# Neighbourhood attention in blocks of 8 rows by 16 columns, keys in chunks of 4 rows, and one value product for both row halves

## The chip, the core and the metric

One Trainium2 chip, one of its cores. Five engines run side by side, each from its own queue in order: TensorE (PE, with its weight loads shown as PEld), VectorE (DVE), ScalarE (ACT), GpSimd (POOL) and SyncE (SP, which here only issues DMAs; ACT and POOL issue some too). The metric is the device time of one execution in microseconds (us), the median of three runs.

## The reference, cut to what matters

One encoder layer on 1024 tokens of 1024 channels: an input projection, three branches (a Fourier mix, neighbourhood attention, attention into 256 memory tokens), a gated merge, an output projection, a LayerNorm, and then a mixture of 64 experts. The change is inside neighbourhood attention. The tokens are a grid of 16 rows by 64 columns; each of 8 heads has 64 channels; a query attends to a window of 8 rows by 16 columns that is clipped at the grid's edges, with a learned bias for each offset:

```
col_start = np.clip(cols - NA_COL_WIN // 2, 0, GRID_W - NA_COL_WIN)
...
def one_row(r):
    rs = jnp.clip(r - kr // 2, 0, rows - kr)
    k_win = k_rows[:, :, :, col_idx]; v_win = v_rows[:, :, :, col_idx]
    sc = jnp.einsum('bhcd,bhrckd->bhcrk', q_r, k_win) * scale + bias
    p = softmax over the 8 x 16 keys
    return jnp.einsum('bhcrk,bhrckd->bhcd', p, v_win)
```

## The kernel before

Everything is float32. Projections run as three products of split operands (high and low parts, `xh`, `xl`, `wh`, `wl`): method `job` issues 48 matmuls of 512 columns for each 128 output channels (L195), in two halves of 512 tokens; a `sink` takes each half out of PSUM. The projections wait in one list (`js`); `adv(n)` issues the next n of their matmuls, `finish(name)` issues all up to the end of one job. So projection matmuls of later work (gates, memory queries) fill PE between the steps of attention.

Method `na` runs the neighbourhood attention. First the four V jobs, whose sink (`v_sink`, L489) copies V out of PSUM (`vt`), turns it by transposes on PE (L503) and lays it into `V`. Then, for each pair of heads `hp`, the Q and K jobs; `q_sink` (L518, L519) splits Q into a high part by ACT and a low part by DVE, `k_sink` does so for K and copies halves by DMA. Then units: a unit is one head `a` of the pair and one block of 128 queries. Before, a block is 4 rows by 32 columns, and its keys are 8 or 11 rows by 40 columns; there are 64 units. A unit has these steps:

- `scores`: two matmuls over all of the block's keys (high and low K, L562) of 320 or 440 columns into a bank `s`; DVE adds bias and mask and takes the minimum (L568), ACT takes the exponential (L570), DVE the reciprocal and the product (L571, L572), into `sc`;
- `turned`: transposes of `sc` on PE (L583), one for each chunk of keys (3 rows, 2 rows or 1 row of 40 columns, so 120, 80 or 40 keys; 3, 3, 4, 4, 5, 5, 3, 3 of them for the eight units of a half row), into a bank `t`, and copies into `pt`, one for each size of chunk, by ACT and DVE in turn (`evac`, L151, L153);
- `values`, once for two units (both heads): for each chunk and each head one product of 128 columns with V as the stationary operand (L598), into a bank `o`. The two heads stand in different halves of the array's columns (64 each). The program has 240 such products; the trace shows each as two instructions.

Between `scores` and `turned` and after `turned` stand `adv(3)` each. `na_bias` loads the bias by a DMA on ACT's queue and POOL subtracts it from the masks (L540, L541), a half row ahead. `tile` schedules the whole program beforehand with its own estimates, so that the order in which instructions stand on an engine is not the order of the code.

What follows attention: the memory attention with the rest of the projections as filler, `merge`, `out_proj` with routing, and the experts, whose weights (64 times three of 2 MB) come by DMA.

Of the kernel before, what the change touches and what calls it, by code (L numbers as in the profile page):

```python
# [5 lines left out]
F32 = mybir.dt.float32  # L6
# [5 lines left out]
OP = mybir.AluOpType  # L12
# [7 lines left out]
KF = 516  # L20

# [14 lines left out]
def constants():  # L36
# [27 lines left out]
    q, kc = np.arange(32), np.arange(40)  # L64
    m = np.arange(-4, 8)
    i = np.arange(4)
    cm = np.zeros((2, 4, 32, 40))
    for h in range(2):
        cs = np.clip(32 * h + q - 8, 0, 48)
        cm[h] = np.where((24 * h + kc >= cs[:, None]) & (24 * h + kc < cs[:, None] + 16), 0.0, 1e30)  # L70
    rm = np.where((m >= i[:, None] - 4) & (m < i[:, None] + 4), 0.0, 1e30)
    c["nmask"] = cm.reshape(2, 128, 1, 40).astype(np.float32)
    mid = np.maximum(cm[:, :, :, None, :], rm[None, :, None, :11, None])
    c["nmask_mid"] = mid.reshape(2, 128, 11, 40).astype(np.float32)
# [3 lines left out]
def layout(i):  # L78
# [17 lines left out]
    q, kc, hf = np.arange(32), np.arange(40), np.arange(2)  # L96
    dc = np.clip((24 * hf[:, None, None] + kc) - (32 * hf[:, None, None] + q[:, None]) + 15, 0, 30)
    dr = np.arange(-4, 8) - np.arange(4)[:, None] + 7
    g = rpb[:, dr[None, :, None, :, None], dc[:, None, :, None, :]]
    a["rpb"] = np.ascontiguousarray(g.reshape(8, 2, 128, 12, 40))  # L100
# [22 lines left out]
class Dense:  # L123
# [304 lines left out]
    def fourier_merge(s, pool):  # L428
# [24 lines left out]
        for d in range(8):  # L453
# [14 lines left out]
            for b in range(2):  # L468
# [13 lines left out]
    CHUNKS = ((0, 3), (3, 3), (8, 3), (11, 3), (4, 2), (6, 2), (14, 2))  # L482

    BLOCKS = ((0, 8, ((0, 3), (1, 3), (5, 2))),
# [3 lines left out]

    def v_sink(s, f):  # L489
        def sink(half, p):  # L490
            v = s.N1.tile([128, 2, 320], F32, name="vt", bufs=2)
            for hf in range(2):
                s.evac(v[:, hf].rearrange("p (r c) -> p r c", c=40), p.rearrange("p (r c) -> p r c", c=64)[:, :, 24 * hf:24 * hf + 40])

            def later():
                V = s.V.rearrange("p (h c) f -> p h c f", h=2)
                for cs, K in (((0, 1), 120), ((4, 5), 80)) if half == 0 else (((2, 3), 120), ((6,), 80)):
                    q = s.bank("t")
                    n = len(cs)
                    for hf in range(2):  # L500
                        for i, c in enumerate(cs):
                            r = s.CHUNKS[c][0] - 8 * half
                            s.nc.tensor.transpose(q[:K, (n * hf + i) * 128:(n * hf + i + 1) * 128], v[:, hf, 40 * r:40 * r + K], s.ident)  # L503
                    s.evac(V[:K, :, cs[0]:cs[0] + n, f * 128:(f + 1) * 128],
                           q[:K, :2 * n * 128].rearrange("p (h c f) -> p h c f", h=2, c=n))
            return later
        return sink

    def q_sink(s, hp):
        def sink(half, p):  # L510
            nc = s.nc
            if half == 0:
                s.QS = s.N1.tile([128, 2, 2, 16, 32], FR, name="QS")
            for a in range(2):
                for h in range(2):
                    src = p[64 * a:64 * a + 64].rearrange("p (r h c) -> p h r c", h=2, c=32)[:, h]
                    hi, lo = s.QS[0:64, a, h, 8 * half:8 * half + 8], s.QS[64:128, a, h, 8 * half:8 * half + 8]
                    nc.scalar.activation(hi, src, AF.Copy, scale=-0.125)  # L518
                    nc.vector.scalar_tensor_tensor(lo, src, -0.125, hi.bitcast(F32), op0=OP.mult, op1=OP.subtract)  # L519
        return sink  # L520
# [14 lines left out]
    def na_bias(s, h, hf):  # L535
        nc, A, pool = s.nc, s.A, s.N1
        bt = pool.tile([128, 12, 40], F32, name="bt", bufs=4)
        bm = pool.tile([128, 11, 40], F32, name="bm", bufs=4)
        nc.scalar.dma_start(bt, A["rpb"][h, hf])
        nc.gpsimd.tensor_tensor(out=bm, in0=s.nmm[:, hf], in1=bt[:, 0:11], op=OP.subtract)  # L540
        nc.gpsimd.tensor_tensor(out=bt, in0=s.nm[:, hf].to_broadcast([128, 12, 40]), in1=bt, op=OP.subtract)  # L541
        return bt, bm

    def na(s, fill):

        nc, A, pool = s.nc, s.A, s.N1
        s.nm = pool.tile([128, 2, 1, 40], F32, name="nm")
        nc.scalar.dma_start(s.nm, A["nmask"].rearrange("h p o c -> p h o c"))
        s.nmm = pool.tile([128, 2, 11, 40], F32, name="nmm")
        nc.scalar.dma_start(s.nmm, A["nmask_mid"].rearrange("h p r c -> p h r c"))  # L550
        s.V = pool.tile([120, 14, 512], F32, name="V")
        pend = []
        ev = s.evac

        def scores(u):
            hp, hf, rb, a = u
            k0, nr, _ = s.BLOCKS[rb]
            W = nr * 40
            sp = s.bank("s")
            q = s.QS[:, a, hf, 4 * rb:4 * rb + 4].rearrange("p r c -> p (r c)")  # L560
# [30 lines left out]
        def values(u, pts):  # L591
            hp, hf, rb, _ = u
            ch = s.BLOCKS[rb][2]
            if rb == 0:
                s.po = s.bank("o")
# [1106 lines left out]
```

## Time and profile before

| what | value |
|---|---|
| median of three runs | 1897.42 us (1896.06 to 1897.73) |
| the profiled execution | 1895.74 us, of which the span in the trace is 1893.9 us |
| PE busy | 1827.3 us, 96% |
| DVE, ACT, POOL busy | 685.6, 455.8, 127.8 us |
| DMA | 522.93 MB, 276 GB/s in the mean |

The profile gives stretches, groups of instructions, and who waited for whom. The end of a matmul is modelled: durations of matmuls that follow each other overlap, so what a matmul costs is the time from its start to the next one's start, not its duration.

### The profile page before, as it was taken

How to read it: one execution, taken by the hardware profiler on the slowest of the kernel's cores; microseconds unless marked ns; L12 is line 12 of the kernel's file. 1: busy time of each engine (PE TensorE's matmuls, PEld its weight loads, DVE VectorE, ACT ScalarE, POOL GpSimd, SP SyncE). 2: the span in 40 equal slices, each digit the busy share in tenths (PEclk: the TensorE clock that was granted, in tenths of full speed). 3: DMA queues.
4: the chain of work that ended last, by engine and by line, in shares of the span. 5: the costliest groups of instructions: out<-in, count | busy, mean ns of one | idle time of the engine just before them, and what ended most of it. 6: DMA issues, size and time to landing. Idle time of an engine off the chain costs nothing. (4 is left out here: it accounts for less than half of the span.)

```text
span 1893.9 us, 23738 instructions
## 1 busy us (share of the span) xinstructions
PE 1827.3 (96%) x9554; PEld 1128.6 (60%) x9555; DVE 685.6 (36%) x1610; ACT 455.8 (24%) x867; POOL 127.8 (7%) x124
## 2 busy tenths in 40 slices
PE   8999999999999999999899999999999999999995
PEld 7988888777877777777644444434433343344331
DVE  5343224444443447677622213112221121212212
ACT  4332123333443342121111212112120121111211
POOL 1000100000100000000100101001010010000100
PEclk9999999999999999999999999999999999999998
DMA  7264513223223327662799999999999999999993
GB/s 271 78 195 151 165 45 89 67 94 95 76 84 99 113 100 255 218 237 75 300 419 426 427 426 427 426 420 426 427 427 427 425 428 426 421 428 426 426 427 154
DMA packets 78250, 522.93 MB, mean 276 GB/s; under 512 B 10703, under 2 KB 14943, under 8 KB 53432
## 3 DMA queue, kind: packets, MB, share of 16 engines
q1 hardware_dynamic: 55448, 469.31, 61.4%
q10 hardware_dynamic: 16608, 30.65, 4.9%
q0 software_dynamic: 6080, 21.42, 3.0%
q8 instruction: 76, 1.25, 0.3%
q14 instruction: 38, 0.31, 0.0%
HBM read 489.17 MB, written 32.51 MB: 275 GB/s over the span
## 5 line engine op out<-in xcount | busy, mean ns | idle before, releaser
L1297 PE MATMUL pg<-blk,xT 128*64 128x512 f32 x1024 | 456.5, 599 | 25.3 <-DMA blk<-in_w_exp_up 25.3
L1296 PE MATMUL pg<-blk,xT 128*64 128x512 f32 x1024 | 463.7, 601 | 0.3 <-ACT xT L1386 0.3
L1419 DVE SCALAR_TENSOR_TENSOR yl<-pd,wcol,yh 128x512 fp32r<-128x512 f32 x63 | 47.3, 750 | 669.7 <-ACT yh L1418 669.7
L195 PE MATMUL mm<-xl,wh 128*128 128x512 f32 x672 | 264.9, 394 | 0.0
L195 PE MATMUL mm<-xh,wl 128*128 128x512 f32 x672 | 263.9, 393 | 0.0
L195 PE MATMUL mm<-xh,wh 128*128 128x512 f32 x672 | 263.9, 393 | 0.0
L1297 PEld LDWEIGHTS pg<-blk,xT 128*64 128x64 f32 x1024 | 135.7, 137 | 198.7 <-issue 142.5
L1318 PE MATMUL pd<-blk,hTe 128*64 128x512 f32 x504 | 226.6, 592 | 0.0
L1319 PE MATMUL pd<-blk,hTe 128*64 128x512 f32 x504 | 226.6, 592 | 0.0
L1296 PEld LDWEIGHTS pg<-blk,xT 128*64 128x64 f32 x1024 | 132.8, 137 | 142.2 <-issue 138.1
L1299 ACT ACTIVATE gu<-pg 128x512 f32<-128x512 f32 x64 | 38.2, 597 | 569.3 <-PE pg L1297 569.3
L195 PEld LDWEIGHTS mm<-xh,wh 128*128 128x128 f32 x672 | 126.2, 188 | 25.7 <-issue 0.8
L195 PEld LDWEIGHTS mm<-xl,wh 128*128 128x128 f32 x672 | 126.2, 188 | 25.4 <-issue 1.0
L195 PEld LDWEIGHTS mm<-xh,wl 128*128 128x128 f32 x672 | 126.3, 188 | 25.0
L1319 PEld LDWEIGHTS pd<-blk,hTe 128*64 128x64 f32 x504 | 69.0, 137 | 80.2 <-issue 80.2
L1318 PEld LDWEIGHTS pd<-blk,hTe 128*64 128x64 f32 x504 | 68.9, 137 | 63.2 <-issue 62.5
L146 DVE TENSOR_TENSOR wl<-wr,wh 128x1024 fp32r<-128x1024 f32 (+2 forms) x54 | 65.0, 1205 | 109.9 <-ACT wh L145 99.6
L1418 ACT ACTIVATE yh<-pd,wcol 128x512 fp32r<-128x512 f32 x63 | 43.3, 688 | 176.3 <-PE pd L1319 176.3
L145 ACT ACTIVATE wh<-wr 128x1024 fp32r<-128x1024 f32 (+2 forms) x54 | 55.4, 1027 | 95.4 <-PE mm L195 91.4
L934 PE MATMUL mm<-blk,mh 128*128 128x512 f32 (+1 forms) x272 | 70.9, 393 | 1.0 <-ACT mh L145 1.0
L1371 PE MATMUL tp<-sel,hh 128*128 128x128 f32 x248 | 70.1, 283 | 0.8 <-DVE xT L1374 0.8
L1372 PE MATMUL tp<-sel,hl 128*128 128x128 f32 x248 | 68.1, 275 | 0.0
(371 smaller groups left out, 2487.8 us busy)
## 6 DMA issues: line engine op xcount, KB each, us to landing
blk<-in_w_exp_up SPq DMA_DIRECT2D x63, 2048.0 KB, 37.0
blk<-in_w_exp_gate SPq DMA_DIRECT2D x62, 2048.0 KB, 32.9
blk<-in_w_exp_down SPq DMA_DIRECT2D x62, 2048.0 KB, 38.6
wr<-in_w_g SPq DMA_DIRECT2D x24, 512.0 KB, 3.7
g_dram<-gt ACTq DMA_DIRECT2D x48, 256.0 KB, 2.2
s<-g_dram SPq DMA_DIRECT2D x32, 256.0 KB, 4.0
gt<-g_dram SPq DMA_DIRECT2D x8, 512.0 KB, 4.3
m_dram<-br ACTq DMA_DIRECT2D x8, 512.0 KB, 2.7
```

The lines of the kernel that those rows point to most:

```text
L145: s.nc.scalar.activation(hi, src, AF.Copy)
L146: s.nc.vector.tensor_tensor(out=lo, in0=src, in1=hi.bitcast(F32), op=OP.subtract)
L195: s.nc.tensor.matmul(p[:, :width], st[:, k], x[:, k, c], start=k == 0 and pi == 0, stop=k == NK - 1 and pi == 2)
L934: pin(nc.tensor.matmul(p, (mh, mh, ml)[i][:, k], wo[c.start // 512][i % 2][:, at:at + w], start=j == 0, stop=j == m - 1))
L1296: pin(nc.tensor.matmul(pg[0:64], l, wg[k], start=k == 0, stop=k == 7))
L1297: pin(nc.tensor.matmul(pg[64:128], l, wu[k], start=k == 0, stop=k == 7))
L1318: pin(nc.tensor.matmul(pd[0:64], hT[:, f], wd[f][:, 0:512], start=f == 0, stop=f == 3))
L1319: pin(nc.tensor.matmul(pd[64:128], hT[:, f], wd[f][:, 512:1024], start=f == 0, stop=f == 3))
L1371: pin(nc.tensor.matmul(tp[:, j], hh[:, c], o[:, 0], start=True, stop=False))
L1372: pin(nc.tensor.matmul(tp[:, j], hl[:, c], o[:, 0], start=False, stop=False))
L1418: nc.scalar.activation(yh, pd, AF.Copy, scale=s.wcol[:, e:e + 1])
L1419: nc.vector.scalar_tensor_tensor(yl, pd, s.wcol[:, e:e + 1], yh.bitcast(F32), op0=OP.mult, op1=OP.subtract)
```

## The change

A block of queries is now 8 rows by 16 columns: 4 column blocks, each with its own key columns (`KCOLS`: 24 columns wide for the two at the edges, 32 for the two in the middle), and 2 row halves `hf`, each with 12 rows of keys. There are again 64 units. A unit's scores are 12 x 32 = 384 or 12 x 24 = 288 columns wide. Its keys are cut into 3 chunks of 4 rows (128 or 96 keys), so 3 transposes and one copy into `pt` for each unit. The two row halves share the two middle chunks: `values` runs once for four units (two heads, two halves), and takes those two chunks for both halves in one product of 256 columns, the outer two in products of 128: 128 products in place of 240. V has 16 chunks for each column block set (64 transposes, 56 before), and its sink makes four copies in place of two. The high part of Q is made by one ACT instruction for each head and half in place of two, the low part by four DVE instructions of 128 columns in place of two of 256. The bias and its mask are two tables (`m` for middle blocks, `e` for edge blocks) with both row halves in them, one POOL instruction and one DMA for each head and table; the bias read from HBM is 7.9 MB in place of 3.9 MB.

```diff
+KCOLS = ((0, 24), (8, 32), (24, 32), (40, 24))
...
-    CHUNKS = ((0, 3), (3, 3), (8, 3), (11, 3), (4, 2), (6, 2), (14, 2))
-
-    BLOCKS = ((0, 8, ((0, 3), (1, 3), (5, 2))),
-              (0, 11, ((0, 3), (1, 3), (2, 3), (5, 2))),
-              (4, 11, ((2, 3), (3, 3), (4, 2), (5, 2), (6, 1))),
-              (8, 8, ((2, 3), (3, 3), (6, 2))))
+    ORDER = (1, 2, 0, 3)
...
             def later():
-                V = s.V.rearrange("p (h c) f -> p h c f", h=2)
-                for cs, K in (((0, 1), 120), ((4, 5), 80)) if half == 0 else (((2, 3), 120), ((6,), 80)):
+                for i in (0, 2):
                     q = s.bank("t")
...
             for a in range(2):
-                for h in range(2):
...
+                src = p[64 * a:64 * a + 64].rearrange("p (r b c) -> p b r c", b=4, c=16)
+                hi, lo = s.QS[0:64, a, :, 8 * half:8 * half + 8], s.QS[64:128, a, :, 8 * half:8 * half + 8]
+                nc.scalar.activation(hi, src, AF.Copy, scale=-0.125)
+                for b in range(4):
+                    nc.vector.scalar_tensor_tensor(lo[:, b], src[:, b], -0.125, hi[:, b].bitcast(F32), op0=OP.mult, op1=OP.subtract)
...
+            for i, r in enumerate(((0, 1, 2), (2, 0, 1))[hf]):
+                nc.tensor.transpose(tp[:K, i * 128:(i + 1) * 128], sc[:, r * K:r * K + K], s.ident)
+            ev(pts[a][:K, :, hf], tp[:K, :384].rearrange("p (c f) -> p c f", f=128))
...
-            for i, (c, n) in enumerate(ch):
+            for g, i, c in ((1, 1, slice(0, 2)), (0, 0, slice(0, 1)), (3, 0, slice(1, 2)), (2, 2, slice(0, 2))):
                 for a in range(2):
-                    nc.tensor.matmul(s.po[64 * a:64 * a + 64, rb * 128:(rb + 1) * 128],
-                                     s.V[:40 * n, hf * 7 + c, hp * 128 + 64 * a:hp * 128 + 64 * a + 64],
-                                     pts[a][:40 * n, i], start=i == 0, stop=i == len(ch) - 1)
+                    nc.tensor.matmul(s.po[64 * a:64 * a + 64, j % 2 * 256 + c.start * 128:j % 2 * 256 + c.stop * 128],
+                                     s.V[:K, j, g, hp * 128 + 64 * a:hp * 128 + 64 * a + 64],
+                                     pts[a][:K, i, c].rearrange("p h f -> p (h f)"), start=g == 1, stop=g == 2)
...
-                if old[0][3] == 1:
-                    values(old[0], [pts.pop(old[0][:3] + (a,)) for a in range(2)])
+                if old[0][2:] == (1, 1):
+                    values(old[0])
```

How the instructions stand. On PE, in the second quarter of the first pair of heads, before: value products (`o<-pt,V`), transposes of the weights of attention (`t<-ident,sc`) and scores (`s<-KH,QS`, `s<-KL,QS`) stand like this.

```order
L598 MATMUL o<-pt,V 64x128
L583 MATMUL t<-ident,sc 120x128
L598 MATMUL o<-pt,V 64x128 x7
L583 MATMUL t<-ident,sc 120x128
L583 MATMUL t<-ident,sc 80x128 x2
L583 MATMUL t<-ident,sc 40x128
L562 MATMUL s<-KH,QS 128x320
L562 MATMUL s<-KL,QS 128x320
```

One product of a group stands alone, ahead of the rest; in all of the program before, the 240 products stand in 51 runs, 18 of them of one product alone.

On PE, first pair of heads, after: the run of the first group,

```order
L563 MATMUL s<-KH,QS 128x288
L563 MATMUL s<-KL,QS 128x288
L593 MATMUL o<-pt,V 64x256
L593 MATMUL o<-pt,V 64x128 x4
L593 MATMUL o<-pt,V 64x256 x2
L583 MATMUL t<-ident,sc 128x128 x3
```

and, a little later, the product that stands alone ahead of the second group (L201 is the projection, L195 before):

```order
L593 MATMUL o<-pt,V 64x256
L583 MATMUL t<-ident,sc 96x128 x3
L563 MATMUL s<-KH,QS 128x288
L563 MATMUL s<-KL,QS 128x288
L201 MATMUL mm<-xl,wh 128x512
```

Products of one size became products of two sizes. The 128 products stand in 38 runs: 19 of one product of 256 columns alone, 3 of one of 128 alone, 13 of seven (three of 256 columns, four of 128) and 3 of five (two of 256, three of 128).

On DVE, between the second and the third pair of heads, before: the low parts of Q (`QS`) and K (`KL`), the splits of projection weights (`wl`), and the last copies of the pair.

```order
L519 SCALAR_TENSOR_TENSOR QS<-mm,QS 64x256
L571 RECIPROCAL st<-st 128x1
L572 TENSOR_SCALAR sc<-sc,st 128x320
L519 SCALAR_TENSOR_TENSOR QS<-mm,QS 64x256 x3
L153 COPY pt<-t 80x256
L146 TENSOR_TENSOR wl<-wr,wh 128x1024
L519 SCALAR_TENSOR_TENSOR QS<-mm,QS 64x256 x3
L153 COPY pt<-t 120x256
L519 SCALAR_TENSOR_TENSOR QS<-mm,QS 64x256
L146 TENSOR_TENSOR KL<-mm,KH 64x512 x2
L146 TENSOR_TENSOR wl<-wr,wh 128x1024
L146 TENSOR_TENSOR KL<-mm,KH 64x512 x2
```

And on DVE at the same place after:

```order
L159 COPY pt<-t 96x3x128
L521 SCALAR_TENSOR_TENSOR QS<-mm,QS 64x128 x8
L152 TENSOR_TENSOR wl<-wr,wh 128x1024
L521 SCALAR_TENSOR_TENSOR QS<-mm,QS 64x128 x8
L152 TENSOR_TENSOR KL<-mm,KH 64x512 x2
L152 TENSOR_TENSOR wl<-wr,wh 128x1024
L152 TENSOR_TENSOR KL<-mm,KH 64x512 x2
```

The 8 pieces of Q of a pair became 16 shorter ones, ahead of the same splits of K.

## Rows read from the trace of the kernel before

**Rows 1.** The page: busy time by engine, and DMA in 40 slices of the span.

```profile
PE 1827.3 (96%) x9554; PEld 1128.6 (60%) x9555; DVE 685.6 (36%) x1610; ACT 455.8 (24%) x867; POOL 127.8 (7%) x124
...
DMA  7264513223223327662799999999999999999993
```

**Rows 2.** Busy us by stretch (count): PE, PEld, DVE, ACT, POOL; PE clock, DMA, GB/s.

```profile
232.00:285.00 53.00, 53.00 (x263) 43.92 (x262) 14.19 (x24) 13.27 (x24) 7.08 (x7) 1.00 0.14 47
...
300.00:620.00 320.00, 320.00 (x1834) 254.85 (x1833) 144.13 (x396) 120.00 (x286) 29.09 (x27) 1.00 0.30 91
...
700.00:800.00 100.00, 95.26 (x403) 75.08 (x402) 70.96 (x119) 25.93 (x39) 2.56 (x3) 1.00 0.72 237
...
925.00:1893.90 968.90, 920.18 (x4687) 387.06 (x4687) 225.02 (x485) 165.72 (x267) 75.04 (x52) 0.99 0.97 410
```

**Rows 3.** PE's waits from 225 to 940 us: total us, times, longest.

```profile
PE t L1136 <- DVE M L1129: 5.6, 7, 2.5
...
PE pg L1296 <- ACT xT L1386: 0.3, 1, 0.3
```

**Rows 4.** PE in order of time: start, us, operation, count; scores of 440 columns.

```profile
335.42 0.39 PE L195 MATMUL mm<-xh,wh 128*128 128x512 f32 x1
335.65 0.39 PE L195 MATMUL mm<-xl,wh 128*128 128x512 f32 x1
335.97 1.46 PE L598 MATMUL o<-pt,V 120*64 120x128 f32 x18
337.36 0.87 PE L583 MATMUL t<-ident,sc 128*120 128x128 f32 x6
337.98 0.45 PE L562 MATMUL s<-KH,QS 128*128 128x440 f32 x1
...
338.47 0.39 PE L195 MATMUL mm<-xh,wl 128*128 128x512 f32 x1
```

**Rows 5.** The same view: scores of 320 columns.

```profile
330.01 0.40 PE L562 MATMUL s<-KH,QS 128*128 128x320 f32 x1
...
330.40 0.39 PE L195 MATMUL mm<-xh,wl 128*128 128x512 f32 x1
```

**Rows 6.** The same view: runs of value products of three lengths.

```profile
354.96 0.43 PE L598 MATMUL o<-pt,V 120*64 120x128 f32 x2
355.32 0.32 PE L583 MATMUL t<-ident,sc 128*120 128x128 f32 x1
355.57 1.09 PE L598 MATMUL o<-pt,V 120*64 120x128 f32 x14
356.59 0.65 PE L583 MATMUL t<-ident,sc 128*120 128x128 f32 x4
...
386.14 0.87 PE L598 MATMUL o<-pt,V 120*64 120x128 f32 x10
386.94 0.54 PE L583 MATMUL t<-ident,sc 128*120 128x128 f32 x3
```

**Rows 7.** Groups by line from 300 to 620 us: busy us, mean ns, idle before.

```profile
L598 PE MATMUL o<-pt,V 120*64 120x128 f32 (+2 forms) x480 | 42.4, 283 | 0.0
...
L598 PEld LDWEIGHTS o<-pt,V 120*64 120x64 f32 (+2 forms) x480 | 28.7, 136 | 18.3 <-issue 16.0 <-DVE QS L519 0.7 <-ACT QS L518 0.7
```

**Rows 8.** Groups by line and shape from 232 to 611 us.

```profile
L146 DVE TENSOR_TENSOR wl<-wr,wh 128x1024 fp32r<-128x1024 f32 x25 | 31.7, 1268 | 45.9 <-ACT wh L145 35.9 <-PE t L503 10.0
...
L519 DVE SCALAR_TENSOR_TENSOR QS<-mm,QS 64x256 fp32r<-64x256 f32 x32 | 13.5, 423 | 12.8 <-ACT QS L518 12.5
...
L153 DVE COPY pt<-t 120x384 f32<-120x384 f32 x10 | 5.3, 551 | 1.2 <-PE t L583 1.2
...
L153 DVE COPY pt<-t 40x128 f32<-40x128 f32 x8 | 2.2, 273 | 0.0
```

**Rows 9.** DVE in order of time between two pairs; in brackets its idle time.

```profile
370.41 0.42 DVE L153 COPY pt<-t 120x256 f32<-120x256 f32 x1 [2.95 <-PE t L583]
...
377.22 1.23 DVE L146 TENSOR_TENSOR wl<-wr,wh 128x1024 fp32r<-128x1024 f32 x1 [3.67 <-ACT wh L145]
```

More of the change, by code (lines that the diff above doesn't have):

```diff
@@ L62, in constants @@
     c["l0mask"] = m
[L64 to L67, printed above, removed]
-    for h in range(2):
[L69 to L74, printed above, removed]
+    q = np.arange(128)
+    for n, bs in (("nmask_m", (1,)), ("nmask_e", (0, 3))):
+        m = np.zeros((2, 128, len(bs), 12, KCOLS[bs[0]][1]))
+        for hf in range(2):
+            for i, b in enumerate(bs):
+                c0, w = KCOLS[b]
+                rs = np.clip(8 * hf + q // 16 - 4, 0, 8)[:, None, None]
+                cs = np.clip(16 * b + q % 16 - 8, 0, 48)[:, None, None]
+                kr, kc = 4 * hf + np.arange(12)[:, None], c0 + np.arange(w)
+                m[hf, :, i] = np.where((kr >= rs) & (kr < rs + 8) & (kc >= cs) & (kc < cs + 16), 0.0, 1e30)
+        c[n] = np.ascontiguousarray(m.reshape(2, 128, -1).transpose(1, 0, 2)).astype(np.float32)
     return c
@@ L95, in layout @@
     rpb = np.asarray(i["rpb"])[0]
[L96 to L100, printed above, removed]
+    q = np.arange(128)
+    for n, bs in (("rpb_m", (1,)), ("rpb_e", (0, 3))):
+        g = []
+        for hf in range(2):
+            for b in bs:
+                c0, w = KCOLS[b]
+                dr = 4 * hf + np.arange(12)[None, :, None] - (8 * hf + q // 16)[:, None, None] + 7
+                dc = c0 + np.arange(w)[None, None, :] - (16 * b + q % 16)[:, None, None] + 15
+                g.append(rpb[:, np.clip(dr, 0, 14), np.clip(dc, 0, 30)].reshape(8, 128, -1))
+        a[n] = np.ascontiguousarray(np.concatenate(g, 2))
     fo = np.asarray(i["w_fourier_o"])[0].reshape(4, 128, D)
@@ L610, in na, with biases @@
+            if j == 3:
+                nc.scalar.dma_start(s.o_dram[hp], s.Ot.rearrange("p r b c -> p (r b c)"))
+        def biases(hp, n):
+            for a in range(2):
+                bias[n, a] = s.na_bias(2 * hp + a, n)
+        units = [(hp, j, hf, a) for hp in range(4) for j in range(4) for hf in range(2) for a in range(2)]
+        old = None
         for i in range(len(units) + 1):
@@ L618, in na @@
                 s.adv(16)
-            if u and u[2:] == (0, 0):
-                if u[:2] == (0, 0):
-                    ahead = nxt(0, 0)
-                s.bias = ahead
-                hp, hf = (u[0], 1) if u[1] == 0 else (u[0] + 1, 0)
-                if hp < 4:
-                    ahead = nxt(hp, hf)
+                if hp == 0:
+                    biases(0, "m")
+                biases(hp, "e")
+            if u and u[1:] == (2, 0, 0) and u[0] < 3:
+                biases(u[0] + 1, "m")
             if u:
```

117 lines of the change are left out of this document (49 added, 68 removed).

## The prediction, made before the changed kernel ran

> **What bounds the kernel now.** I read the page first: PE is busy 96% of the span, no other engine over 36%, and the DMA line shows 9 in every slice from the 20th to the 39th and low numbers before [rows 1]. So there are two regimes: PE up to about 925 us, the experts' weights after it. The stretches say the same: from 925 us on DMA has a share of 0.97 and moves 410 GB/s; from 300 to 620 us, where attention runs, PE is busy 320.00 of 320 us, and 53.00 of 53 where V is made, while DVE has 144 and ACT 120 us of 320 [rows 2]. PE's waits from 225 to 940 us fill eight lines, from 5.6 us down to 0.3 us, and none names a line of attention [rows 3]. So in attention PE never waits for softmax, copies or bias: the stage is a queue of PE instructions laid end to end, and its time is the sum of their issue steps. That sum is what the change touches. Everything behind (memory attention, merge, output projection, experts) begins when PE gets there, so a shorter queue moves all of it, and with it the start of the weight stream.
>
> Since matmuls overlap, I price each by the time from start to the next start. A projection matmul takes 0.23 us (335.42 to 335.65) [rows 4]; these stay as they are in number.
>
> **Transposes.** Six of them take 0.62 us (337.36 to 337.98), 0.104 us each [rows 4], though stationary widths are mixed: what moves is always 128 columns. In the loop 240 become 192, for V 56 become 64: 40 fewer, -4.2 us. The widths 96 and 128 that come are between and beside those seen (80 and 120), so the ends are close: -4 to -4.5.
>
> **Scores.** From the high product to the next projection matmul it is 0.49 us for 440 columns (337.98 to 338.47) [rows 4] and 0.39 for 320 (330.01 to 330.40) [rows 5]: two products, 240 columns more, 0.10 us, so 0.42 ns a column. For 384 columns that gives 0.443, for 288 0.363; the mean of a unit falls from 0.440 to 0.403, and 64 units give -2.4 us. If runs of 24 or 32 keys were read more slowly than runs of 40 the gain could be nil; nothing in the rows says so. I take -2.4.
>
> **Value products.** One 128-column product alone takes 0.36 us to the next start (354.96 to 355.32), five take 0.80 (386.14 to 386.94), seven 1.02 (355.57 to 356.59) [rows 6]: 0.25 + 0.11 n. A product has two passes; n products take n+1 steps of 0.11, because the second pass of one head's product runs beside the first pass of the other head's, plus 0.14 for the ends. Before the run the last projection matmul takes 0.32 in place of 0.23 (335.65 to 335.97) [rows 4], 0.09 more. Check on before: 51 runs and 240 products give 51 x 0.34 + 240 x 0.11 = 43.7 us, beside 42.4 us busy in the group's row [rows 7]. After: a step that holds a pass of 256 columns is 0.22. Alone, 256 columns: 0.14 + 2 x 0.22 = 0.58, 19 times, 11.0 us. Seven: 0.14 + 5 x 0.22 + 3 x 0.11 = 1.57, 13 times, 20.4. Five: 0.14 + 3 x 0.22 + 3 x 0.11 = 1.13, 3 times, 3.4. Three of 128 alone: 1.1. Entries: 38 x 0.09 = 3.4. Together 39.3, so -4.4. One more thing goes: before, chunks of 40 keys sit in the middle of longer runs, and the run of nine at 335.97 takes 1.39 us [rows 4] where 0.25 + 9 x 0.11 is 1.24: 0.15 us, 8 such groups of products a kernel, about -1. I take -5. The ends: no product of 256 columns overlaps its neighbour (+7, below), or the ends too shrink as chunks get equal (-8).
>
> **What lies beside PE.** Copies into `pt` fall from 144 to 64; one of 384 columns takes 0.55 us on DVE [rows 8]. Softmax gets narrower. V's sink has four copies in place of two, POOL's bias work is about the same in elements (15360 in place of 14720 a partition), the bias DMAs carry 4 MB more in a stretch that moves 91 GB/s [rows 2]. On DVE the low part of Q goes from 8 pieces to 16 a pair: the old ones took 0.423, the nearest row for 128 elements is a copy of 0.273 [rows 8], so a pair's DVE work grows by between 16 x 0.273 - 8 x 0.423 = 1.0 and 16 x 0.423 - 3.4 = 3.4 us. I take the lower half, nearest in elements. It is priced at nothing, since DVE idles there for 2.95 and 3.67 us at a time, waiting for PE [rows 9], and the splits of K come a job (48 x 0.23 = 11 us) after those of Q; without that cover it costs 4 to 13.6 us in four pairs. By the Trainium skill, VectorE: DVE Perf Modes, "Side-by-side", an instruction carries about 150 cycles beside its elements, which would make a piece about 0.29 us, an estimate; the sum is the same by it.
>
> **Sum.** -4.2 - 2.4 - 5.0 = -11.6 us. The profiled execution, 1895.74 us, would be 1884.1; the median of the runs lies 1.7 above it, so 1885.8, 0.6% less.
>
> **Rivals.** First, **unequal products do not overlap**. The rows show overlap for products of one size only. If a 256-column product runs both passes alone, the 64 cost 0.44 each and the 64 others 0.22: 42.2 us, with 38 x 0.23 for ends and entries 50.9, 7 more than 43.7 in place of 5 less. Sum +0.4: 1898, no change. For it: no row of before has two sizes side by side. Against it: the 0.11 a product comes from passes on different column halves, which don't depend on each other's length. 0.08.
>
> Second, **the copy before the values becomes the end** (the slower one). Now `values` takes all four units of a block at once, behind a single copy of 0.55 us for the last unit, and that copy can stand on DVE behind a split of weights (1.27 us [rows 8]) and a pass of softmax. PE would wait in front of the run, in 16 places. From the order of after, between the last transposes of a group and the product that reads them there are 4.4 us or more of other PE instructions in all 16 groups at the prices above (4.1 to 5.8 in the 32 of before, where PE didn't wait). The chain to cover is 0.55 + 1.27 + 0.6, some 2.4 us. To end slower by 0.2%, PE would have to lose 15.4 us, 1.0 us at each of 16 places, so the chain would have to be 5.4 us. At 1.0 to 1.3 us a place it gives 1902 to 1906. 0.05.
>
> Third, **part of it is given back later**: PE is idle 4.7 of 100 us from 700 to 800 [rows 2], and the scheduler's order there (loads of the output weights on SP, the splits behind them) comes out a little differently. Should those 4.7 us double, 1890.5; should the stage take two thirds of the gain, 1893.5; all of it, 1897. 0.14 for at least half of the gain lost, a third of that from 1893.6 up.
>
> Fourth, **weight loads cost PE time**. In the run of seven 14 instructions start within 1.02 us [rows 6], 0.073 each, while a weight load of these products lasts 0.136 in the mean [rows 7]: loads are hidden. If they were not, in two column halves side by side, 480 x 0.136 / 2 = 32.6 of the 42.4 us would be loads, 224 of 480 would go, 15.2 us, and the sum would be about -22: 1875. The Trainium skill, TensorE: Matmul & The Clock Gate, Part 3 ("What overlaps and what doesn't"), says weight loads overlap running matmuls only where the row groups differ, which here they don't; by that rule it is this rival; the trace speaks against it. 0.03.
>
> **How the numbers follow.** The forecast, PE's queue shorter by 8 to 15 us: 0.70, 1885.8, between 1881 (value term -8, V and transposes at their better ends) and 1890. Rivals 0.08, 0.05, 0.14, 0.03. About 0.2% (3.8 us) is what a measurement here can tell from none: faster than 1893.6 takes the forecast, the fourth and two thirds of the third, 0.82; within 0.2% the first and most of the rest of the third, 0.12; slower 0.06. The range reaches from 1880 to 1895: below it the fourth and a little of the forecast, above it the first two and the third's last part.
>
> **What would show it.** PE busy in all of attention's stretch, about 12 us shorter, no line of attention among PE's waits; transposes at 0.104; runs of seven in 1.57 us (2.3 or more would be the first rival); 0.40 for a mean pair of scores; a gap in front of `o<-pt,V` put down to `pt` would be the second; the first expert load, and the end, earlier by as much as attention's end, or else the third. It would be wrong if narrow runs of keys slow the scores, or if the stage behind waits for something other than PE.

## The result: 1886.9 us, and the profile of the changed kernel

The changed kernel takes 1886.9 us (median of five runs, 1883.4 to 1889.3), beside 1896.1 us for the kernel before on the same chip: a ratio of 0.9948, interval 0.9936 to 0.9960, so 7.6 to 12.1 us less. The prediction was 1885.8 us. The profiled execution took 1888.03 us with a span of 1886.3 us; that of before took 1895.74 us with 1893.9.

The page of after, busy time by engine and the DMA line in 40 slices, answers to [rows 1]:

```profile
PE 1819.5 (96%) x9290; PEld 1116.2 (59%) x9291; DVE 678.4 (36%) x1610; ACT 445.8 (24%) x819; POOL 126.5 (7%) x108
...
DMA  7254513323233237652799999999999999999993
```

PE has lost 264 matmuls and 7.8 us of busy time; DVE has as many instructions as before. The DMA line still has two regimes.

The stretches of after (columns as in [rows 2]: PE, PEld, DVE, ACT, POOL with counts, granted clock of PE, DMA share, GB/s):

```profile
300.00:610.00 310.00, 310.00 (x1579) 243.50 (x1579) 135.91 (x389) 110.97 (x242) 28.78 (x15) 1.00 0.33 106
...
688.00:700.00 12.00, 10.19 (x38) 7.83 (x37) 7.32 (x8) 6.60 (x8) 0.00 (x0) 0.86 0.86 320
700.00:743.00 43.00, 42.52 (x183) 33.95 (x181) 30.11 (x55) 10.53 (x17) 0.00 (x0) 1.00 0.75 248
743.00:753.00 10.00, 7.18 (x20) 5.39 (x19) 6.87 (x13) 3.04 (x5) 0.00 (x0) 0.66 0.80 255
753.00:790.00 37.00, 36.22 (x156) 28.87 (x155) 24.08 (x41) 5.38 (x8) 2.56 (x3) 1.00 0.51 162
```

In attention PE is busy for 310.00 of 310 us at the full clock, as before. New is what stands behind POOL's column from 688 us on, where merge begins: a granted clock of 0.86 and of 0.66. Merge before had 1.00 throughout; the stretches of before that answer to the two:

```profile
700.00:712.00 12.00, 10.79 (x44) 7.78 (x43) 7.76 (x9) 6.98 (x9) 0.00 (x0) 1.00 0.85 312
...
754.00:764.00 10.00, 8.84 (x39) 6.97 (x38) 7.41 (x14) 3.05 (x5) 0.00 (x0) 1.00 0.76 233
```

PE's waits from 225 to 925 us, longest sum first (total us, times, longest), answer to [rows 3]:

```profile
PE t L1133 <- DVE M L1126: 5.6, 7, 2.5
PE pg L167 <- ACT gh L151: 5.1, 3, 2.8
...
PE pg L1293 <- ACT xT L1383: 0.3, 1, 0.3
```

No line of attention is among them. The second row is merge: its products (`pg`) wait three times for the high part of a gate's weights (`gh`). Before they waited three times as well, for less:

```profile
PE pg L161 <- ACT gh L145: 3.8, 3, 1.4
```

The table follows the change down the program, by the ends and starts of single instructions on PE in the profiled executions. "Span end less merge end" is the output projection and the experts.

| us | before | after | difference |
|---|---|---|---|
| last projection matmul ends | 700.7 | 688.6 | -12.1 |
| first merge product starts | 703.6 | 690.4 | -13.2 |
| merge, first to last product | 92.8 | 98.0 | +5.1 |
| span end less merge end | 1097.5 | 1097.9 | +0.4 |
| span | 1893.9 | 1886.3 | -7.6 |

The expectations below count merge from the last projection matmul (95.7 us before, 99.8 after); before, memory attention's last products still lie in between, so here it is counted from merge's own first product.

So 13.2 us came out of the stage that the change touches, 5.1 of them went in merge, and nothing after that.

**Where the 13 us come from.** The table adds, for each kind of PE instruction up to the first merge product, the time from its start to the next start in the trace (the price that the prediction used). A wait counts on the instruction ahead of it.

| us, start to next start | before | after | predicted difference | measured |
|---|---|---|---|---|
| value products `o<-pt,V` | 38.9 | 33.9 | -5 with the step ahead | -5.0 |
| transposes of attention `t<-ident,sc` | 25.0 | 18.0 | -5.0 | -7.0 |
| transposes of V `t<-ident,vt` | 5.0 | 5.9 | +0.8 | +0.9 |
| scores, high and low K | 25.9 | 23.9 | -2.4 | -2.0 |
| projections, 2064 matmuls | 482.9 | 485.0 | 0 | +2.1 |
| memory attention, `o<-mpt,vm` | 14.3 | 12.5 | 0 | -1.8 |
| all PE instructions | 698.8 | 685.7 | -11.6 | -13.1 |

The rows of projections and memory attention hold the wait ahead of the first merge product. Before, it stands behind a memory product, whose step is 1.80 us where others take 0.43; after, behind a projection, whose step is 2.20 us where others take 0.23. With these two steps at the price of the others memory attention differs by -0.4 us and the projections by +0.1.

Three rows of after in order of time (start, us, operation, count; a product shows as two records) answer to [rows 4 to 6]:

```profile
327.24 0.65 PE L593 MATMUL o<-pt,V 128*64 128x256 f32 x2
327.82 0.55 PE L583 MATMUL t<-ident,sc 128*128 128x128 f32 x3
...
329.38 1.51 PE L593 MATMUL o<-pt,V 128*64 128x256 f32 x14
330.82 0.55 PE L583 MATMUL t<-ident,sc 128*128 128x128 f32 x3
...
382.15 1.08 PE L593 MATMUL o<-pt,V 96*64 96x128 f32 x10
383.17 0.45 PE L563 MATMUL s<-KH,QS 128*128 128x384 f32 x1
```

A lone product of 256 columns takes 0.58 us, as predicted; the run of seven 1.44, not 1.57; the run of five 1.02, not 1.13.

### The profile page after: what moved, and what is told of

The parts are those of the page before. It is cut to its first block, busy times and chain, and to the rows that moved or that the text cites. A ratio compares the mean times of both kernels' runs of the same rounds, so it can differ in the third digit from the quotient of the medians.

```text
span 1886.3 us, 23170 instructions
## 1 busy us (share of the span) xinstructions
PE 1819.5 (96%) x9290; PEld 1116.2 (59%) x9291; DVE 678.4 (36%) x1610; ACT 445.8 (24%) x819; POOL 126.5 (7%) x108
## 3 DMA queue, kind: packets, MB, share of 16 engines
q8 instruction: 74, 1.21, 0.3%
## 5 line engine op out<-in xcount | busy, mean ns | idle before, releaser
L201 PE MATMUL mm<-xl,wh 128*128 128x512 f32 x672 | 266.2, 396 | 0.0
L201 PE MATMUL mm<-xh,wh 128*128 128x512 f32 x672 | 265.1, 394 | 0.0
L201 PE MATMUL mm<-xh,wl 128*128 128x512 f32 x672 | 264.3, 394 | 0.0
L201 PEld LDWEIGHTS mm<-xh,wh 128*128 128x128 f32 x672 | 126.4, 188 | 25.5 <-issue 0.9
L201 PEld LDWEIGHTS mm<-xl,wh 128*128 128x128 f32 x672 | 126.4, 188 | 25.3 <-issue 1.6
L201 PEld LDWEIGHTS mm<-xh,wl 128*128 128x128 f32 x672 | 126.4, 188 | 25.0 <-issue 0.9
```

The source lines that it names most:

```text
L201: s.nc.tensor.matmul(p[:, :width], st[:, k], x[:, k, c], start=k == 0 and pi == 0, stop=k == NK - 1 and pi == 2)
```

## The experiments

The first theory was that of the prediction: PE's queue sets attention's time, every PE instruction counts at its own step, and what merge gave back came from longer waits there. Each kernel below is one small edit. The marks are those of the profiled executions in us; a median is that of all runs of a kernel, compared with the kernel before in the same set.

| kernel | last projection ends | first merge product | last merge product | merge | span | median | ratio to before (interval) |
|---|---|---|---|---|---|---|---|
| before | 700.7 | 703.6 | 796.4 | 92.8 | 1893.9 | 1896.1 | |
| after | 688.6 | 690.4 | 788.4 | 98.0 | 1886.3 | 1886.9 | 0.9948 (0.9936 to 0.9960) |
| after_b | 688.6 | 690.4 | 786.0 | 95.6 | 1884.4 | 1886.4 | 0.9943 (0.9930 to 0.9955) |
| vsplit | 692.4 | 694.2 | 787.2 | 93.0 | 1884.8 | 1887.8 | 0.9959 (0.9945 to 0.9972) |
| va10 | 677.6 | 679.4 | 778.0 | 98.6 | 1881.9 | 1876.2 | 0.9888 (0.9872 to 0.9903) |
| tr4 | 696.2 | 698.0 | 793.7 | 95.7 | 1890.1 | 1893.0 | 0.9981 (0.9972 to 0.9990) |
| m1 | 688.6 | 690.4 | 780.8 | 90.4 | 1877.0 | 1882.4 | 0.9929 (0.9915 to 0.9942) |
| b10 | 691.0 | 694.2 | 788.8 | 94.6 | 1885.4 | 1884.0 | 0.9928 (0.9915 to 0.9942) |
| bm1 | 701.2 | 704.1 | 794.0 | 89.9 | 1892.2 | 1892.6 | 0.9977 (0.9968 to 0.9986) |
| best | 676.7 | 678.6 | 771.0 | 92.4 | 1868.9 | 1870.4 | 0.9858 (0.9843 to 0.9873) |
| bbest | 690.3 | 693.4 | 788.0 | 94.5 | 1893.5 | 1892.2 | 0.9979 (0.9967 to 0.9990) |
| ev2 | 683.5 | 686.4 | 781.3 | 95.0 | 1884.4 | 1882.7 | 0.9921 (0.9906 to 0.9937) |
| q2 | 689.7 | 691.5 | 788.5 | 97.0 | 1886.0 | 1887.6 | 0.9944 (0.9930 to 0.9959) |

### vsplit: the products of 256 columns cut in two again

```diff
-            for g, i, c in ((1, 1, slice(0, 2)), (0, 0, slice(0, 1)), (3, 0, slice(1, 2)), (2, 2, slice(0, 2))):
-                for a in range(2):
-                    nc.tensor.matmul(s.po[64 * a:64 * a + 64, j % 2 * 256 + c.start * 128:j % 2 * 256 + c.stop * 128],
...
+            for h in range(2):
+                for g, i in ((1, 1), (3 * h, 0), (2, 2)):
+                    for a in range(2):
+                        nc.tensor.matmul(s.po[64 * a:64 * a + 64, (j % 2 * 2 + h) * 128:(j % 2 * 2 + h + 1) * 128],
...
```

> The changed kernel with the products of the two middle chunks split again, one for each row half: 192 value products of 128 columns in place of 64 of 256 and 64 of 128. The columns are the same (24,576); the planner cuts them into 57 unbroken runs in place of 38. Theory (a run of value products costs TensorE 0.25 us at its edges and 0.11 us for each 128 columns): 57 x 0.25 + 192 x 0.11 = 35.4 us of value products against 38 x 0.25 + 192 x 0.11 = 30.6, so the last projection matmul ends 4.8 us later than in the changed kernel (688.6 -> 693.4), and the end comes about as much later if the merge stage is left as it is. Rival (only columns cost, or wide products cost more than narrow ones because the two column halves then don't overlap): no change or a gain, the last projection matmul at 688.6 or before.

The last projection matmul came 3.7 us later, not 4.8, and not 0. The value products themselves add up to 33.9 us, to the tenth what they take in after: 192 narrow products cost what 64 wide and 64 narrow ones cost. What grew is what stands at the edges of the 57 runs: the transposes (18.0 to 21.4 us) and the projections (485.0 to 487.0). A transpose ahead of a run of products takes 0.20 us to the next start and one ahead of a score or a projection 0.03; 21 stand ahead of a run here, 5 in after. That the products cost the same is a balance, by the law that va10 shows below: 19 runs more add 2.7 us, and the column half that sets a run's length has 117 pieces of 128 columns in place of 131, mostly since the products left alone are narrow (3.1 us less). So the theory's 4.8 us was nearly met for another reason, and a wide product is by itself no cheaper than two narrow ones; it saves runs. By the medians little of the 3.7 us is left (1887.8 beside 1886.9); in the profiled executions merge took 93.0 us in place of 98.0.

The rows that settle weight loads stand here too: groups by line from 300 to 620 us (count, busy us, mean ns, idle before), after first and vsplit second.

```profile
L593 PEld LDWEIGHTS o<-pt,V 128*64 128x64 f32 (+1 forms) x256 | 18.9, 136 | 12.3 <-issue 9.6 <-DVE sc L572 1.1 <-ACT sc L570 0.7
```

```profile
L594 PEld LDWEIGHTS o<-pt,V 96*64 96x64 f32 (+1 forms) x384 | 24.1, 136 | 15.6 <-issue 13.8 <-DVE st L568 0.7 <-DVE sc L572 0.7
```

128 more weight loads of 136 ns, 17.4 us if they stood end to end, added nothing to the 33.9 us. They overlap each other too: their busy time grew by 5.2 us.

### va10: head 1's products issued first

```diff
-                for a in range(2):
+                for a in (1, 0):
```

> The changed kernel with the two heads' value products issued in the other order (head 1 first). The planner then has no lone 256-column product to put ahead of the others for 13 of 16 groups: 22 runs of value products in place of 38, with the same products in all. Theory (0.25 us for each run's edges): 16 x 0.25 = 4.0 us less, and by the changed kernel's own rows (lone product 0.58, run of seven 1.44, so a run of eight at 1.44 + 0.22 = 1.66) 13 x 0.36 + 3 x 0.36 = 5.8 us less: the last projection matmul ends at 682.8 to 684.6 in place of 688.6. Rival (the lone product fills a wait that would otherwise stand on TensorE, for the copy of the second head's probabilities): TensorE waits at the run instead, about 0.3 us for each of 13, and nothing is gained.

The last projection matmul came 11.0 us earlier, twice what was expected, and PE has no wait in attention. The row of va10 that shows why is its run of eight products, in order of time on PE:

```profile
341.31 0.39 PE L201 MATMUL mm<-xh,wl 128*128 128x512 f32 x1
341.62 1.52 PE L593 MATMUL o<-pt,V 128*64 128x256 f32 x16
343.08 0.64 PE L583 MATMUL t<-ident,sc 128*96 128x128 f32 x4
```

Eight products take 1.46 us; seven took 1.44 in after. The eighth is free. In after the planner issues one head's first product alone (why it does was not looked into), and that head's other products then run beside the other head's; the lone one costs 0.58 us with nothing beside it on the other half of the columns, and the run behind it doesn't get shorter, because the other head's half is the longer one. So the price of the prediction, 0.25 + 0.11 n, is only the mean of a better law: **a run takes 0.14 us, and 0.22 us for each 128 columns of the column half that has more of them**. A lone product of 128 columns: 0.36. Five of 128 (three on one half): 0.80; seven: 1.02 [rows 6]. Lone 256: 0.58. After's seven (halves of 768 and 512 columns) and va10's eight (768 and 768): 0.14 + 6 x 0.22 = 1.46 each. After's five (512 and 384): 1.02. A nine of before, 1.24 by it, takes 1.39 [rows 4], the 0.15 that the prediction had noticed: each run that holds a chunk of 40 keys (8 in each kernel with the tiling of before) takes 0.15 more. All other runs of the thirteen profiles lie within 0.02 us of the law. In va10 sixteen lone runs less make the value products 25.4 us in place of 33.9; the law gives 13 x 0.58 + 3 x 0.36 = 8.6 for that difference, and 8.5 was measured. The other 2.5 us are the steps beside the runs (projections -1.9). The profiled execution is the slowest of va10's four (1872.1 to 1883.8 us): behind the router PE waits 6.15 us for `hTe`, where neither before nor after waits, so the span shows 4.4 us less than after's where the medians show 10.7.

### b10: the same edit in the kernel before

Its diff is va10's, in the `values` of the kernel before.

> The kernel before with the two heads' value products issued in the other order (head 1 first). The planner then makes 34 runs of value products (18 of three pairs, 8 of four, 6 of five, 2 of two) in place of 51 with 18 lone products; the 240 products are the same. Theory (the two heads' products, on the two column halves, run side by side, so a run costs 0.14 us + 0.22 us for each pair of 128 columns, a lone product as much as a pair, and 0.09 us on the step ahead of it): 34 x 0.23 + 120 x 0.22 = 34.2 us against 38.9 + 51 x 0.09 = 43.5, so 9.3 us less: the last projection matmul at 691.4 in place of 700.7, and about 1888 at the end. The change itself is then worth less than 3 us on top of this at that mark (688.6 with its own lone products), and 13.8 us once both have no lone product (677.6). Rival (what the other order gained in the changed kernel, 11 us, comes from the products of 256 columns alone, or from something else that the planner moved): 3 us or less.

691.0, where 691.4 was expected. Value products fell from 38.9 to 32.6 us. A run of three pairs in b10 (six products, twelve records), in order of time on PE:

```profile
341.80 0.37 PE L562 MATMUL s<-KH,QS 128*128 128x440 f32 x1
342.10 0.88 PE L598 MATMUL o<-pt,V 120*64 120x128 f32 x12
342.91 0.76 PE L583 MATMUL t<-ident,sc 128*120 128x128 f32 x5
```

0.81 us, the 0.80 of a run of five [rows 6]. So the lone products cost the kernel before nearly as much as the changed one (9.7 us at that mark, 11.0 there), and by the medians (0.9928 beside 0.9948, intervals that overlap) this edit of one line is worth about as much as the whole change. It also says what the change is worth with it: at the last projection matmul 13.4 us (b10 to va10), beside 12.1 without (before to after) and 12.6 with the edit to merge below in both (bm1 to m1); at the end, by the ratios of va10 and b10, about 7.6 us. Against the rival, the gain isn't bound to products of 256 columns.

### tr4: a fourth transpose in each unit

```diff
                 nc.tensor.transpose(tp[:K, i * 128:(i + 1) * 128], sc[:, r * K:r * K + K], s.ident)
+            nc.tensor.transpose(tp[:K, 384:512], sc[:, 0:K], s.ident)
```

> The changed kernel with a fourth transpose of 128 columns behind the three of each unit, into a part of the PSUM bank that nothing reads (redundant work): 64 more transposes. Theory (one transpose in a run costs TensorE 0.104 us and nothing hides it): the last projection matmul ends 64 x 0.104 = 6.7 us later (688.6 -> 695.3). Rival (a transpose is hidden beside other work of TensorE, or the run's edges are the whole cost): 0 to 2 us later.

7.6 us later at that mark, 0.119 us for each transpose, and 6.1 us in the median: they are paid in full, a little above the 0.104 of the prediction's row. The rival falls.

### ev2 and q2: DVE's and ACT's work doubled

```diff
+            s.flip ^= 1
+            ev(pts[a][:K, :, hf], tp[:K, :384].rearrange("p (c f) -> p c f", f=128))
```

> The changed kernel with the copy of the transposed probabilities into pt made twice, one behind the other on the same engine (redundant work, 64 copies more of 0.5 to 0.6 us on DVE or ACT): it doubles what the second rival of the prediction feared. Theory (TensorE has 4.4 us or more of other instructions between the last transposes of a group and the products that read the copies): no wait of TensorE at o<-pt,V, the last projection matmul within 1 us of 688.6, the end unchanged but for merge. Rival (the copy stands close to the end of the chain): waits at o<-pt,V in 16 places, 0.3 to 0.6 us each, 5 to 9 us in all.

```diff
-                for b in range(4):
+                for b in (0, 1, 2, 3) * 2:
```

> The changed kernel with the low part of Q computed twice (redundant work: 64 pieces of 64x128 more on DVE, ahead of the splits of K and the weights). Theory (DVE idles there, and TensorE has other work until Q and K are wanted): no wait of TensorE in attention, the last projection matmul within 1 us of 688.6. Rival (the cover is gone, and the pieces delay the scores of the next pair): 4 to 13.6 us in four pairs, shown as waits at s<-KH,QS.

PE's stretch of attention in ev2 and in q2, columns as above:

```profile
300.00:600.00 300.00, 300.00 (x1547) 236.98 (x1546) 150.52 (x412) 121.17 (x265) 28.31 (x14) 1.00 0.33 102
```

```profile
300.00:610.00 310.00, 310.00 (x1579) 243.52 (x1578) 147.69 (x433) 111.12 (x241) 28.89 (x15) 1.00 0.33 106
```

PE waits for nothing in either, with twice the copies and twice the pieces of Q. Both kinds of work are covered. For ev2 the expected mark was wrong all the same: 683.5, 5.1 us earlier, since the two copies changed the planner's order, in which 14 lone wide products are left of 19 and 33 runs of 38. For q2 the mark moved by 1.1 us. That extra, useless work makes attention end earlier in one of two cases says how much the order alone is worth here.

### m1, bm1 and after_b: what merge gave back

Merge in after, in order of time: ScalarE first, then PE. The bracket is the idle time before, with what ended it.

```profile
738.44 0.63 ACT L151 ACTIVATE blk<-gr 128x512 fp32r<-128x512 f32 x1 [1.56 <-DMA gr<-in_w_out]
740.27 0.63 ACT L151 ACTIVATE blk<-gr 128x512 fp32r<-128x512 f32 x1 [1.20 <-DMA gr<-in_w_out]
743.29 0.63 ACT L151 ACTIVATE blk<-gr 128x512 fp32r<-128x512 f32 x1 [2.39 <-DMA gr<-in_w_out]
744.92 0.63 ACT L151 ACTIVATE blk<-gr 128x512 fp32r<-128x512 f32 x1 [1.00 <-DMA gr<-in_w_out]
745.46 0.61 ACT L151 ACTIVATE gh<-gr 128x512 fp32r<-128x512 f32 x1
```

```profile
688.23 0.39 PE L201 MATMUL mm<-xh,wl 128*128 128x512 f32 x1
690.42 3.43 PE L167 MATMUL pg<-Om,gh 128*128 128x512 f32 x8 [1.81 <-ACT gh L151]
...
742.92 0.39 PE L167 MATMUL pg<-On,gl 128*128 128x512 f32 x1
746.12 2.07 PE L167 MATMUL pg<-Om,gh 128*128 128x512 f32 x4 [2.82 <-ACT gh L151]
```

The split that PE wants at 743.3 stands on ScalarE behind four splits of output weights (`blk<-gr`), each waiting for its own load; its own load had been issued at 733.30. Behind the 1.81 us the record of the granted clock shows 0.5 (1.2 GHz in place of 2.4) from 690.9 for 3.4 us, behind the 2.82 us from 745.5 for 6.8 us; the products of merge take twice as long there (eight in 3.43 us). Half of 3.4 is 1.7, half of the 6.2 us of work in the second is 3.1: an estimate of 4.8 us for the clock. The waits inside merge are 0.48 + 2.82 us in place of 1.16 + 1.41 before, 0.7 more. Together 5.5, beside the 5.1 that merge lost: nearly all of it is the clock, little of it longer waiting.

```diff
-            for k in range(2 * d - 2, 2 * d) if 0 < d < 5 else ():
+            for k in (d,):
```

> The changed kernel with the loads and splits of the output projection's weights, in the merge stage, spread evenly over the eight steps (one row block of w_out for each step in place of two in steps 1 to 4), so that ScalarE has never more than three of them ahead of a split that the merge products wait for. Attention is untouched. Theory (about 4.6 us of the gain were given back in merge, since TensorE waited 2.82 us behind four such splits and then ran at 1.2 GHz for 6.83 us): the long wait and the half clock behind it go, the last merge product ends 3 to 4.5 us earlier against the last projection matmul (99.8 us behind it in the changed kernel, 95.7 in the kernel before), and the end comes 3 to 4.5 us earlier, near 1882 to 1883. Rival (merge is bound by its loads, and a shorter wait at one place comes back at another): less than 1 us.

> The kernel before with the loads and splits of the output projection's weights spread evenly over the eight steps of merge. Theory (what this edit gave the changed kernel was the wait of 2.82 us and the half clock behind it, which the kernel before does not have): the last merge product comes 92 to 94.5 us behind the last projection matmul in place of 95.7, a gain of 1 to 3.5 us against 7.6 in the changed kernel's profile; the end near 1893 to 1895. Rival (two row blocks of weights a step are a burden to merge in either kernel, and the change gave nothing back there): as much as in the changed kernel's runs, 4.5 us or more, 1892 or less.

> The changed kernel as it is, once more, for a second profiled execution. Theory (the two long waits in merge come from the order of instructions on ScalarE and SyncE, so every execution has them): TensorE waits 1.81 us behind the last projection matmul and 2.8 us some 55 us later, the clock falls to 1.2 GHz behind the second and mostly behind the first, the last merge product is 98 to 100 us behind the last projection matmul. Rival (the second wait was an accident of transfers in one execution): no wait above 1.5 us in the middle of merge, 93 to 96 us.

The stretches of m1 that answer to those of after above:

```profile
688.00:700.00 12.00, 10.19 (x44) 7.98 (x43) 7.34 (x8) 6.60 (x8) 0.00 (x0) 1.00 0.88 321
...
743.00:753.00 10.00, 10.00 (x44) 8.10 (x43) 6.82 (x14) 2.15 (x4) 0.00 (x0) 1.00 0.77 248
```

The wait in the middle is gone, the clock is full, and merge takes 90.4 us, 7.6 less. In the kernel before the same edit takes merge from 92.8 to 89.9. With it in both, merge is as long in one as in the other, and all that attention gains is there when merge ends: 794.0 against 780.8. That is the theory's side. But two things speak against putting the whole 5.1 us on the order. In m1 the wait of 1.81 us is still there and the clock stayed full behind it; and the second execution of the changed kernel, after_b, has these rows on PE:

```profile
741.71 0.40 PE L167 MATMUL pg<-On,gl 128*128 128x512 f32 x1
744.24 1.51 PE L167 MATMUL pg<-Om,gh 128*128 128x512 f32 x4 [2.14 <-ACT gh L151]
745.55 1.05 PE L167 MATMUL pg<-On,gh 128*128 128x512 f32 x2
```

The same wait is 2.14 us, the half clock follows it, but the wait of 1.81 us at 688.6 passed without one, and merge took 95.6 us (97.4 behind the last projection matmul, where 98 to 100 was expected). Of the 2.7 us that merge lost in this execution 0.9 are waits (3.4 in place of 2.6 us) and 1.7, by the same estimate, the clock. So the order of instructions explains 0.7 to 0.9 us as waiting in either execution, and the rest, 4.8 in one and 1.7 in the other, came and went with the clock. By the medians the edit is worth 3.6 us in the changed kernel (0.9948 to 0.9929 of 1896) and 4.4 in the kernel before, nearer to the rival's number for bm1 (4.5) than to the theory's (1 to 3.5). By the same ratios the change is worth 9.9 us with the edit in neither kernel and 9.1 with it in both: the times don't show that the loss in merge belongs to the change. Runs of one kernel lie some 5 us apart (m1: 1878.7 to 1884.1), in va10 12, so the medians don't decide between 3 and 7; the profiles do for the wait, and leave the clock open.

### best and bbest: both edits together

> The changed kernel with both: value products issued head 1 first, and the weights of the output projection spread over the steps of merge. Theory (the two edits act in different stages and add up): the last projection matmul at 677.6 as with the first alone, the last merge product 92 us behind it as with the second alone, 770 in all, 18 us before the changed kernel; the end at 1870 to 1873. Rival (the stream of the experts' weights behind takes the gain, since it can't start earlier or ends by its own pace): no earlier than 1876, the time of the first edit alone.

> The kernel before with both edits: value products issued head 1 first, and the weights of the output projection spread over the steps of merge. Theory (the edits add up here as in the changed kernel): last projection matmul at 691.0, last merge product 92 to 94 us behind it, the end 4 us under the 1884.0 of the first edit alone: 1879 to 1881. The changed kernel with both (1870.4) is then 9 to 11 us better: what the change itself is worth where neither kernel has a lone product and both have the same merge; by the marks it should be 14 (691.0 against 676.8). Rival (what is left of the change beside the pairing is lost behind merge): bbest at 1875 or less.

In the changed kernel they add up: the last merge product at 771.0, and 1870.4 us, 1.4% under before and 0.9% under the changed kernel; the stream of the experts' weights starts and ends that much earlier. In the kernel before they don't. The last projection matmul is near the expected mark (690.3), but the last merge product comes 97.7 us behind it, where 92 to 94 was expected: merge takes 94.5 us, b10's 94.6, so the second edit gives merge nothing there. And the median is 1892.2, 8 us above b10. PE's waits of bbest from 755 to 800 us:

```profile
PE mm L934 <- ACT mh L145: 6.1, 1, 6.1
PE pg L161 <- DVE gl L146: 2.9, 1, 2.9
```

The 2.9 us for `gl` stand inside merge, with half clock behind them for 3.4 us; b10 has the same (2.6 us and 3.4). Then PE stands for 6.1 us between merge and the output projection, where the kernel before waits 1.0, and the clock is at 0.5 from 790.1 for 6.8 us, 2.8 of them behind the wait. What `mh` waits for is the last of DVE's adds, and they wait for the last loads of a gate from `g_dram`, which SyncE issues only at 787.72, as merge's products end (787.95):

```profile
787.72 1.71 SPq L731 DMA_DIRECT2D s<-g_dram  x3
```

```profile
790.41 0.69 DVE L736 SCALAR_TENSOR_TENSOR s<-s,pg 128x512 f32<-128x512 f32 x1 [1.32 <-DMA s<-g_dram]
```

In before these loads start 6.1 us ahead of merge's end. ev2, without the edit to merge, has a like wait of 4.3 us, and there these loads start 2.0 us ahead of merge's end, so the edit is not the only way to it; why the load comes so late was not taken apart. The comparison of best with bbest is therefore not a measure of the change.

## Why the prediction was right, and where it wasn't

**What bounds the kernel: right.** PE is full in attention in all thirteen profiles, no line of attention is among its waits, and 64 transposes more or 16 lone runs less moved the end of the stage by what they cost.

**The sum: right in size, -11.6 predicted and -13.1 measured.** The step "everything behind begins when PE gets there" held up to the first merge product (-13.2), and again from merge's end to the span's end (+0.4). That the end came within 1.1 us of the forecast is partly luck: attention gave 1.5 us more than the sum, merge took 5.1 that the forecast had at nothing, and the kernel before was at 1896.1 in this set of runs, 1.4 below the 1897.4 that the forecast starts from. By the medians the gain is 9.2 us where 11.6 was forecast.

**Value products: right total, wrong law.** The term's size, -5, was met (38.9 to 33.9), but by two misses that offset each other: the working has 35.9 us of products after (39.3 less 3.4 for entries), 2.0 too many, and the further -1 for runs of nine comes off a price that already held them (51 x 0.25 + 240 x 0.11 = 39.2 for before, 38.9 measured). "n products take n+1 steps of 0.11" is the price of a run in which both heads have about equally many columns. The run of seven was mis-sized at 1.57 (1.44), the run of five at 1.13 (1.02), and the prediction didn't see that of the 19 lone wide products 13 were waste: with the other head's beside them they cost nothing. That is the largest thing it missed, 11 us in va10, and it lay in [rows 6] already: one product at 0.36 and five at 0.80 are one step and three, not one and five.

**Transposes: mis-sized.** -4.2 with those of V, -6.1 measured. The loop's went from 0.104 to 0.094 us each. Counted in the two traces, a transpose followed by a score or a projection shows 0.03 us to the next start; 47 of 240 stood so before, 53 of 192 now, which makes some 1.4 of the 1.9 us. tr4's further ones cost 0.119.

**Scores: -2.4 predicted, -2.0 measured.** A mean pair went from 0.40 to 0.37 us, where the working had 0.44 and 0.40: the level was off, the difference nearly right. Narrower runs of keys are read no more slowly.

**Steps priced at nothing.** Projections took 2.1 us more and memory attention 1.8 less; that is nearly all the wait ahead of merge, 1.21 us before and 1.81 after, which changed its row. So 0.6 us of PE's queue was a wait that grew. Q's pieces cost nothing, as predicted: q2 shows the cover. They take 0.283 us each on DVE. The Trainium skill, VectorE: DVE Perf Modes, "Side-by-side", had given an estimate of 0.29 us; the trace agrees.

**First rival, unequal products don't overlap: falls.** 1.44 us for the run of seven, where it asked for 2.3.

**Second rival, the copy ahead of the values: falls.** No wait at `o<-pt,V`, even with each copy made twice.

**Third rival, part given back later: came true in part.** 5.1 of 13.2 us in the profiled execution, 2.7 in the second, less than the half that it was priced for. The sign that the prediction named for it came: the first expert load is 8.1 us earlier (798.9 to 790.8), not 12.1. The place was right (merge, loads and splits of the output weights), the mechanism only half named: the waits in merge grew by 0.7 to 0.9 us, and the clock behind them took the rest. The prediction had priced longer waits, not a slower PE.

**Fourth rival, weight loads cost PE time: falls.** By the Trainium skill, TensorE: Matmul & The Clock Gate, Part 3, loads overlap running matmuls only where row groups differ. Here rows are the same and only column halves differ, and 128 further loads in vsplit cost no product time: its 57 runs take 33.9 us, and a law without a term for loads gives 33.7. The trace doesn't agree with the rule, and the measurement decides.

**What stays open.** Why the clock falls behind a wait of 1.81 us in some executions and not in others, and so how much of the merge's loss belongs to the change. Also why runs with a chunk of 40 keys take 0.15 us more, and why bbest and ev2 load the last gate so late.

## What to carry to other kernels

Products that use different column halves of the array run beside each other only if the queue puts them next to each other, so a run costs what its longer half costs: look for lone products, and turn the order of issue before rebuilding the tiling. A gain in a stage that one engine bounds moves the start of the next stage in full, but a planner reorders that stage too, and a wait there can cost more through the clock behind it than by itself. So follow the gain by marks from stage to stage, and price the change by the medians of several executions as well as by one profile; to even out the next stage in both kernels didn't give a clean price here (bbest).

## What the hardware showed that was not expected

A product on the other column half is free if its neighbour in the queue is on the longer half: eight products in 1.46 us, seven in 1.44, one of 256 columns alone 0.58.

The granted clock after an idle stretch of PE isn't the same from run to run. The wait of 1.81 us ahead of the first merge product stands in eight of the profiles; the clock fell to 1.2 GHz behind it in six of them (after, va10, vsplit, tr4, best, q2) and not in two (m1, after_b). Waits in merge of 2.18, 1.86 and 2.49 us in va10 passed at 2.4 GHz, one of 2.82 in after did not, and the wait of 2.45 us for the router's mask after the output projection was followed by 1.2 GHz in all thirteen. No wait of merge up to 1.6 us was followed by it.
